# First layer norms in groups: one chain of vector instructions for the deviations of several token tiles

## The chip, the cores and the metric

The kernel runs on one core of one Trainium2 chip. Its engines work side by side, each through a queue of its own: PE (TensorE, matmuls and transposes into PSUM), DVE (VectorE), ACT (ScalarE), POOL (GpSimd) and SP (SyncE, which here only issues DMAs). The metric is the device time of one execution in microseconds (us). It was 1414.79 us before (median of three runs, 1411.76 to 1419.1).

## What is computed

One layer of a hybrid decoder over 1024 tokens of width 1024, with 256 memory tokens. Cut to what matters here:

```python
def layer_norm(x, g, b):
    mu = jnp.mean(x, axis=-1, keepdims=True)
    xc = x - mu
    var = jnp.mean(xc * xc, axis=-1, keepdims=True)
    return xc * lax.rsqrt(var + LN_EPS) * g + b

h = layer_norm(x, emb_ln_g, emb_ln_b)          # (1024, 1024): the first norms
mem_n = layer_norm(mem, mem_ln_g, mem_ln_b)    # (256, 1024)
z = h @ w_in                                   # feeds an S5 and a gated linear attention group
...                                            # output projection, cross-attention to mem_n, MLP
```

Everything after `z` (two mixers, cross-attention, a squared-ReLU MLP, three more norms) stays as it is.

## The kernel before

**Tiles.** Tokens lie in tiles of 128: eight of the sequence (`xs`, four to each of two arrays of 128 x 4 x 1024) and two of the memory (`mrow[:, 2]` and `mrow[:, 3]`). A tile has one token per partition and its 1024 features along the row. A mean or a deviation of such a tile is one number per partition: a column of 128 x 1.

**One norm.** `norm_stats` (line 211) reads the two halves of a tile with `bn_stats` (128x512 each), joins them with `bn_aggr` into `mv` (mean, variance), and calls `rsqrt1` (line 172), which finds the reciprocal root by a first guess in integers and three Newton steps: 2 `tensor_scalar` and 6 `scalar_tensor_tensor`, eight instructions of 128x1 that each need the one before. They write the tile `tq`; in the profile they stand as `tq<-mv` (first), `tq<-tq` int32 (second) and `tq<-tq` (the six). `layer_norm` (line 224) then applies it: on DVE (x - mean) * g, then * rstd + b for the left half; for the right half ACT scales with `tq` (for a "light" tile, seven of the eight by `LIGHT = 191`, with a bias that one more small DVE instruction, `tq<-mv,tq`, makes first), and POOL multiplies by g and adds b (`xs<-xs,row`).

**What surrounds it.** `embed(tk)` (line 461) normalises token tile tk, transposes its eight 128x128 blocks on PE, splits them into two parts of reduced precision (`h0T`: ACT the upper part, DVE the rest from PSUM), and stores the tile. `z_block` (line 413) multiplies a token tile by the weights `wr` on PE, 24 matmuls of 128x512; its epilogue `r_epi` uses ACT, DVE and POOL (`rt`). The loops at lines 470 and 505 run `embed(tk)` and `z_block(tk - 1)` in turn for eight tiles; the first four x tiles are loaded before, the next four within these loops. The norms of the memory (line 264) come first of all; then `mem_stream` (line 369) computes head 0 of the memory's projections, in which `mem_proj` splits `kvT` (ACT upper part, DVE the rest).

After the eight tiles come the projection of the gate's rank (line 525), `z_block(7)`, the weights `wu` (line 529; `weight`, line 190, loads `raw`, ACT makes the upper part `hl`, DVE or POOL the rest), and on DVE the parameters of the S5 group (lines 547 to 690, many instructions of 128x16 on `prm` and `par`). `par` takes the buffer of the rows g and b of the first norm, so that its first write waits for the last `xs<-xs,row`. The first product with `wu` is `z_fm` (line 873).

**What sets the order.** Tile dependencies are turned into semaphores, and the order of the instructions of each engine is laid out when the program is built, by program order and by the builder's own estimate of when operands are ready. So a queue holds small instructions of later code in what the builder took for gaps: in the trace the eight-instruction chains of two or three token tiles lie interleaved with other work. At run time each queue is worked through strictly in that order.

Of the kernel before, what the change touches and what calls it, by code (L numbers as in the profile page):

```python
# [7 lines left out]
F32 = mybir.dt.float32  # L8
F32R = mybir.dt.float32r
I32 = mybir.dt.int32  # L10
U8 = mybir.dt.uint8
AF = mybir.ActivationFunctionType
ALU = mybir.AluOpType
# [4 lines left out]
P = 128  # L18
D = 1024
SEQ = 1024  # L20
NT = SEQ // P
# [5 lines left out]
EPS = 1e-5  # L27
# [8 lines left out]
LIGHT = 191  # L36
# [45 lines left out]
def hybrid_layer(  # L82
# [9 lines left out]
    V = nc.vector  # L92
# [4 lines left out]
    x, mem, out = x[0], mem[0], out[0]  # L97
# [18 lines left out]
    small = ctx.enter_context(tc.tile_pool(name="small", bufs=4))  # L116
# [7 lines left out]
    def slot(name, shape, dtype=F32):  # L124
        return arena.tile(shape, dtype, tag="s", name=name)

    def bank(tag="d", shape=(P, 512)):
        return psp.tile(list(shape), F32, tag=tag, bufs={"d": 3, "s": 3, "g": 2}[tag], name="ps_" + tag)
# [6 lines left out]
    def ts(e, o, i, s1, s2=None, op0=ALU.mult, op1=None):  # L135
        if s2 is None:
            e.tensor_scalar(out=o, in0=i, scalar1=s1, scalar2=None, op0=op0)
        else:
            e.tensor_scalar(out=o, in0=i, scalar1=s1, scalar2=s2, op0=op0, op1=op1)  # L139

    def tt(e, o, a, b, op):
        e.tensor_tensor(out=o, in0=a, in1=b, op=op)  # L142

    def stt(e, o, a, s, b, op0, op1):
        e.scalar_tensor_tensor(out=o, in0=a, scalar=s, in1=b, op0=op0, op1=op1)  # L145

    def act(o, i, f=AF.Copy, **kw):
        A.activation(out=o, in_=i, func=f, **kw)  # L148
# [23 lines left out]
    def rsqrt1(y, v, eps, t):  # L172

        vh, w = t[:, 0:1], t[:, 1:2]
        ts(V, vh, v, eps, -0.5, ALU.add, ALU.mult)
        ts(V, y.bitcast(I32), vh.bitcast(I32), -0.5, 1597463007.0 - 2.0 ** 30 - 2.0 ** 22, ALU.mult, ALU.add)
        for _ in range(3):
            stt(V, w, y, vh, y, ALU.mult, ALU.mult)
            stt(V, y, w, 1.5, y, ALU.add, ALU.mult)

    ident = const.tile([P, P], F32, name="ident")
    G.memset(ident, 0.0)
    G.affine_select(out=ident, in_=ident, compare_op=ALU.not_equal, fill=1.0, base=0,
# [19 lines left out]
    def ln_rows(g, b):  # L203
        r = rowp.tile([P, 2, D], F32, tag="row", name="row")
        for i, v in enumerate((g, b)):
            if len(v.shape) == 1:
                v = v.rearrange("(o n) -> o n", o=1)
            nc.sync.dma_start(out=r[:, i, :], in_=v.to_broadcast([P, D]))
        return r

    def norm_stats(xt, st=None):

        mv = small.tile([P, 2], F32, tag="mv", name="mv")
        tq = small.tile([P, 4], F32, tag="tq", name="tq")
        half_done = st is not None
        if not half_done:
            st = small.tile([P, 2, 6], F32, tag="st", name="st")
        for i in range(1 if half_done else 0, 2):
            V.bn_stats(out=st[:, i, :], in_=xt[:, i * 512:(i + 1) * 512])
        V.bn_aggr(out=mv, in_=st)  # L220
        rsqrt1(tq[:, 0:1], mv[:, 1:2], EPS, tq[:, 1:3])
        return mv, tq

    def layer_norm(xt, rows, light=False, st=None):
        mv, tq = norm_stats(xt, st)
        lo_, hi_ = slice(0, 512), slice(512, D)
        if light:
            stt(V, xt[:, lo_], xt[:, lo_], mv[:, 0:1], rows[:, 0, lo_], ALU.subtract, ALU.mult)
            stt(V, tq[:, 3:4], mv[:, 0:1], -1.0, tq[:, 0:1], ALU.mult, ALU.mult)
            act(xt[:, hi_], xt[:, hi_], AF.Identity, scale=tq[:, 0:1], bias=tq[:, 3:4])  # L230
            tt(G, xt[:, hi_], xt[:, hi_], rows[:, 0, hi_], ALU.mult)
        else:
            stt(V, xt, xt, mv[:, 0:1], rows[:, 0, :], ALU.subtract, ALU.mult)
            act(xt[:, hi_], xt[:, hi_], scale=tq[:, 0:1])
        stt(V, xt[:, lo_], xt[:, lo_], tq[:, 0:1], rows[:, 1, lo_], ALU.mult, ALU.add)
        tt(G, xt[:, hi_], xt[:, hi_], rows[:, 1, hi_], ALU.add)

    def transposes(src_ap, dst):

        for b in range(2):  # L240
            pt = bank("s", (P, 4, P))
            for j in range(4):
                PE.transpose(pt[:, j, :], src_ap(4 * b + j), ident)
            hi, lo = dst(b)
            split(hi, lo, pt)
# [3 lines left out]
    mrow = slot("mrow", [P, 4, D])  # L249
# [11 lines left out]
    PE.transpose(gps[:, 0:16], gbr, ident[0:16, 0:16])  # L261
    act(gb, gps[:, 0:16])
    mps = [bank("sssd"[i], (P, 2, MEM)) for i in range(4)]
    for mt in range(2):
        xm = mrow[:, 2 + mt, :]
        mv, tq = norm_stats(xm)
        ts(V, xm[:, 0:512], xm[:, 0:512], mv[:, 0:1], tq[:, 0:1], ALU.subtract, ALU.mult)
        stt(V, tq[:, 3:4], mv[:, 0:1], -1.0, tq[:, 0:1], ALU.mult, ALU.mult)
        act(xm[:, 512:D], xm[:, 512:D], AF.Identity, scale=tq[:, 0:1], bias=tq[:, 3:4])
        for k in range(8):  # L270
            PE.transpose(mps[k // 2][:, k % 2, mt * P:(mt + 1) * P], xm[:, k * P:(k + 1) * P], ident)
    for b in range(4):
        z = (b + 1) % 3 * 512 + 512
        t = mrow[:, 0:2, :].rearrange("p a n -> p (a n)")[:, z:z + 512].rearrange("p (k m) -> p k m", k=2)
        for j in range(2):
            k = 2 * b + j
            if MT >> k & 1:
                act(t[:, j, :], mps[b][:, j, :], AF.Identity, scale=gb[:, k:k + 1], bias=gb[:, 8 + k:9 + k])
            else:
# [11 lines left out]
                  in_=lst[64:80, :].unsqueeze(2).to_broadcast([16, 2, 64]))  # L291
# [142 lines left out]
    xs = [slot("xs0", [P, 4, D])]  # L434
# [3 lines left out]
    rows = ln_rows(emb_ln_g, emb_ln_b)  # L438
# [12 lines left out]
    def r_epi(t, po):  # L451
# [6 lines left out]
        tt(eng(RE, t), th_, th_, ng, ALU.mult)  # L458
        srs.append(lambda: nc.scalar.dma_start(out=sr_d[t * P:(t + 1) * P, :], in_=th_))

    def embed(tk):
        xt = xs[tk // 4][:, tk % 4, :]
        layer_norm(xt, rows, LIGHT >> tk & 1)
        transposes(lambda k: xt[:, k * P:(k + 1) * P],
                   lambda b: tuple(h0T[b][hl][:, :, tk * P:(tk + 1) * P] for hl in range(2)))
        nc.scalar.dma_start(out=h0_d[tk * P:(tk + 1) * P, :], in_=xt)
# [3 lines left out]
    for tk in range(3):  # L470
        embed(tk)
        load_x(tk + 4)
        if tk == PP:
            pps = bank("g")
            PE.transpose(pps[:, 0:P], pm, ident)
            act(prm_s[:, 0:96], pps[:, 0:96])
            act(bglu, pps[:, 96:100], scale=0.5)
            act(bgate, pps[:, 100:102])

            cps = bank("g", (P, 2, 4, 64))  # L480
            for ri in range(2):
                for i in range(4):
                    for g in range(2):
                        PE.matmul(cps[64 * g:64 * g + 64, ri, i, :], cn[:, ri, i, :],
                                  ident.rearrange("p (j g h) -> p g j h", g=2, h=SH)[:, g], start=True, stop=True)
            act(prm_s[:, 2432:2944], cps.rearrange("p r i n -> p (r i n)"))
        if tk:
            z_block(wr, tok_block, tk - 1, r_epi)
# [85 lines left out]
    def exp_parts(z):  # L574

        zc, n, r, em, sc, kk = etmp
        ex, ex1 = pt(), pt()
        ts(e, zc, z, 88.0, -90.0, ALU.min, ALU.max)
        ts(e, n, zc, LOG2E, MAGIC, ALU.mult, ALU.add)
        ts(e, n, n, MAGIC, op0=ALU.subtract)  # L580
        stt(e, r, n, -LN2H, zc, ALU.mult, ALU.add)
        stt(e, r, n, -LN2L, r, ALU.mult, ALU.add)
        ts(e, em, r, 1.0 / 5040)
        for c in (1.0 / 720, 1.0 / 120, 1.0 / 24, 1.0 / 6, 0.5, 1.0):
            stt(e, em, em, c, r, ALU.add, ALU.mult)
# [15 lines left out]
    step, _ = exp_parts(ls)  # L601
# [35 lines left out]
    n = 1  # L637
# [311 lines left out]
    for s in LEVELS + (P,):  # L949
        w = 2 * SEQ // s  # L950
# [759 lines left out]
```

## Time and profile before

| | |
|---|---|
| median of three runs | 1414.79 us |
| the profiled execution: its own time, and the span from first to last instruction in it | 1412.6 us, 1410.8 us |
| mean granted TensorE clock in it | 0.986 |
| ACT, POOL busy | 570.1 us (40%), 460.0 us (33%) |
| moved over DMA | 199.81 MB, 142 GB/s |

The profile is of one execution. In the lists of instructions each row gives start, length, engine, line, operation, written tile <- read tiles, shape and count, and in brackets how long the engine had stood idle before and what released it. Most elementwise instructions are recorded in short helpers (L135 to L148), so groups are told apart by the names of their tiles. A window row gives, for each engine, busy time and count of instructions in a stretch of the span, then the granted clock of PE (1.00 is full speed), the share of the DMA engines and GB/s.

### The profile page before, as it was taken

The numbers are of one execution on the slowest core, as the hardware profiler recorded it, in microseconds if no ns is written. First come the engines' busy times: TensorE is split into PE (matmuls) and PEld (weight loads), VectorE is DVE, ScalarE is ACT, GpSimd is POOL, SyncE is SP. The second block draws the span as 40 slices with busy tenths as digits, with TensorE's granted clock in tenths as the row PEclk, the third lists the DMA queues.
The fourth block names the chain that finished last, engine by engine and source line by source line (L and its number), as shares of the span: only waits on it lengthen the run. The fifth ranks groups of instructions, "written<-read, shape, count | busy, mean of one in ns | idle before, by whom it ended". The sixth has DMA issues, their size and how long they took to land. (4 is left out here: it accounts for less than half of the span.)

```text
span 1410.8 us, 18927 instructions
## 1 busy us (share of the span) xinstructions
PE 1341.5 (95%) x6824; PEld 1112.6 (79%) x6824; DVE 998.0 (71%) x1783; ACT 570.1 (40%) x946; POOL 460.0 (33%) x338
## 2 busy tenths in 40 slices
PE   7798999999899998999998999999999999999997
PEld 6575788788898887788887777778888888888886
DVE  8999588756855489844478667766555676568797
ACT  4433532342545143333123654445545343335431
POOL 1663144312855133200014223443332142003364
PEclk9899999999999999999999999999999999999999
DMA  9722342543756120310120656554446985334432
GB/s 311 255 110 81 107 121 52 161 159 112 255 186 209 56 73 23 119 30 1 60 60 23 194 174 198 194 188 142 145 140 230 343 270 178 104 105 150 149 105 90
DMA packets 155513, 199.81 MB, mean 142 GB/s; under 512 B 16294, under 2 KB 86044, under 8 KB 155292
## 3 DMA queue, kind: packets, MB, share of 16 engines
q1 hardware_dynamic: 143536, 179.44, 39.5%
q10 hardware_dynamic: 11884, 19.17, 3.7%
q8 instruction: 54, 0.88, 0.3%
q14 instruction: 39, 0.32, 0.1%
HBM read 140.38 MB, written 58.20 MB: 141 GB/s over the span
## 5 line engine op out<-in xcount | busy, mean ns | idle before, releaser
L163 PE MATMUL ps_d<-xt,w1q 128*128 128x512 f32 x576 | 138.3, 391 | 9.8 <-DVE w1s L142 9.5
L163 PEld LDWEIGHTS ps_d<-xt,w1q 128*128 128x128 f32 x576 | 107.3, 188 | 35.4 <-issue 12.2
L142 POOL TENSOR_TENSOR hl<-raw,hl 128x1024 fp32r<-128x1024 f32 x21 | 63.0, 3006 | 168.3 <-ACT hl L148 168.2
L163 PE MATMUL ps_s<-cell 128*128 128x512 f32 x432 | 113.0, 389 | 0.0
L163 PE MATMUL ps_d<-cell 128*128 128x512 f32 x432 | 106.0, 389 | 0.4 <-DVE hid L142 0.4
L142 POOL TENSOR_TENSOR R<-R,row 128x512 f32<-128x512 f32 x42 | 57.8, 1386 | 138.4 <-ACT R L148 134.9
L163 PE MATMUL ps_d<-h0T,hl 128*128 128x512 f32 x384 | 93.6, 402 | 5.8 <-DVE hl L142 5.8
L163 PE MATMUL ps_g<-xb,w1q 128*128 128x512 f32 x384 | 94.3, 397 | 3.9 <-ACT hid L148 3.9
L163 PE MATMUL ps_d<-hl,y 128*128 128x512 f32 x384 | 95.1, 403 | 2.5 <-DVE y L142 2.5
L163 PEld LDWEIGHTS ps_d<-cell 128*128 128x128 f32 x432 | 81.0, 188 | 17.6 <-DVE hid L142 0.8
L163 PEld LDWEIGHTS ps_s<-cell 128*128 128x128 f32 x432 | 81.1, 188 | 16.8
L163 PEld LDWEIGHTS ps_d<-h0T,hl 128*128 128x128 f32 x384 | 73.2, 193 | 25.8 <-DVE hl L142 6.2
L163 PE MATMUL ps_d<-hl,h0T 128*128 128x512 f32 x384 | 91.1, 393 | 1.4 <-DVE h0T L142 1.3
L148 ACT ACTIVATE hl<-raw 128x1024 fp32r<-128x1024 f32 x62 | 64.8, 1059 | 66.1 <-PE ps_d L163 60.2
L163 PE MATMUL ps_d<-hl,p 128*128 128x512 f32 x384 | 89.0, 391 | 0.0
L163 PEld LDWEIGHTS ps_g<-xb,w1q 128*128 128x128 f32 x384 | 72.5, 191 | 19.6 <-ACT hid L148 4.7
L163 PEld LDWEIGHTS ps_d<-hl,y 128*128 128x128 f32 x384 | 72.6, 193 | 18.0 <-DVE y L142 3.0
L148 ACT ACTIVATE hid<-hid 128x512 f32<-128x512 f32 x112 | 70.8, 632 | 36.9 <-DVE hid L142 35.1
L163 PEld LDWEIGHTS ps_d<-hl,h0T 128*128 128x128 f32 x384 | 71.0, 188 | 17.3 <-DVE h0T L142 1.8
L163 PEld LDWEIGHTS ps_d<-hl,p 128*128 128x128 f32 x384 | 71.6, 188 | 14.6
L142 DVE TENSOR_TENSOR cell<-ha,cell 128x1024 fp32r<-128x1024 f32 x56 | 78.2, 1401 | 5.6 <-ACT cell L148 3.4
L148 ACT ACTIVATE w1q<-raw 128x512 fp32r<-128x512 f32 x80 | 50.0, 628 | 76.2 <-PE ps_d L163 39.6
(286 smaller groups left out, 2868.8 us busy)
## 6 DMA issues: line engine op xcount, KB each, us to landing
g_d<-hid SPq DMA_DIRECT2D x112, 256.0 KB
ha<-g_d SPq DMA_DIRECT2D x56, 512.0 KB
raw<-in_w_ff_dram SPq DMA_DIRECT2D x40, 512.0 KB
b<-in_w_ff_dram SPq DMA_DIRECT2D x32, 512.0 KB
raw<-in_w_mkv_dram SPq DMA_DIRECT2D x16, 512.0 KB
raw<-in_w_in_dram SPq DMA_DIRECT2D x16, 512.0 KB
wq<-in_w_mq_dram SPq DMA_DIRECT2D x8, 512.0 KB
xs<-in_x_dram SPq DMA_DIRECT2D x8, 512.0 KB
```

The costliest lines, as they stand in the source:

```text
L142: e.tensor_tensor(out=o, in0=a, in1=b, op=op)
L148: A.activation(out=o, in_=i, func=f, **kw)
L163: PE.matmul(o, lhs(i), rhs(j), start=first and n == 0, stop=last and n == 2, skip_group_check=more)
```

## The change

A second helper, `rsqrt_n`, does for n columns (128 x n) what `rsqrt1` does for one. A column cannot be the scalar operand of all n, so the fused instruction `y * vh * y` becomes two `tensor_tensor`: 2 `tensor_scalar`, 6 `tensor_tensor` and 3 `scalar_tensor_tensor`, eleven instead of eight. `norms_stats` makes the `bn_stats` and `bn_aggr` of several tiles (counts and shapes as before), then one such chain. It is called for the two memory tiles, and in `embed` at token tiles 0, 2 and 4, for tiles 0 and 1, 2 and 3, and 4 to 7. The later norms of the kernel go on calling `norm_stats`.

```diff
+    def rsqrt_n(y, v, eps, t):
+        n = y.shape[1]
+        vh, w = t[:, 0:n], t[:, n:2 * n]
+        ts(V, vh, v, eps, -0.5, ALU.add, ALU.mult)
+        ts(V, y.bitcast(I32), vh.bitcast(I32), -0.5, 1597463007.0 - 2.0 ** 30 - 2.0 ** 22, ALU.mult, ALU.add)
+        for _ in range(3):
+            tt(V, w, y, y, ALU.mult)
+            tt(V, w, w, vh, ALU.mult)
+            stt(V, y, w, 1.5, y, ALU.add, ALU.mult)
...
+    def norms_stats(xts):
+        n = len(xts)
+        mv = small.tile([P, 16], F32, tag="dg", bufs=2, name="mvn")[:, 0:8].rearrange("p (t c) -> p t c", c=2)
+        tq = small.tile([P, 12], F32, tag="sq", name="tqn")
+        for k, xt in enumerate(xts):
+            st = small.tile([P, 2, 6], F32, tag="st", name="st")
+            for i in range(2):
+                V.bn_stats(out=st[:, i, :], in_=xt[:, i * 512:(i + 1) * 512])
+            V.bn_aggr(out=mv[:, k], in_=st)
+        rsqrt_n(tq[:, 0:n], mv[:, 0:n, 1], EPS, tq[:, 4:4 + 2 * n])
+        return [(mv[:, k, 0:1], tq[:, k:k + 1], tq[:, 4 + k:5 + k]) for k in range(n)]
...
+    mem_known = norms_stats([mrow[:, 2 + mt, :] for mt in range(2)])
     for mt in range(2):
         xm = mrow[:, 2 + mt, :]
-        mv, tq = norm_stats(xm)
...
     def embed(tk):
         xt = xs[tk // 4][:, tk % 4, :]
-        layer_norm(xt, rows, LIGHT >> tk & 1)
+        if tk not in known:
+            same = range(tk, NT) if tk >= 4 else (tk, tk + 1)
+            known.update(zip(same, norms_stats([xs[i // 4][:, i % 4, :] for i in same])))
+        layer_norm(xt, rows, LIGHT >> tk & 1, known=known[tk])
```

In `layer_norm` the mean, the reciprocal root and the bias column are passed in as `known`; what it does with them is unchanged. The buffers of the new tiles are those of two tags that are next used much later (lines 1085 and 1166).

More of the change, by code (lines that the diff above doesn't have):

```diff
@@ L222, in norm_stats, with layer_norm @@
         return mv, tq
-    def layer_norm(xt, rows, light=False, st=None):
-        mv, tq = norm_stats(xt, st)
+    def norms_stats(xts):
[9 more added lines that the diff above has]
+        return [(mv[:, k, 0:1], tq[:, k:k + 1], tq[:, 4 + k:5 + k]) for k in range(n)]
+    def layer_norm(xt, rows, light=False, st=None, known=None):
+        if known is None:
+            mv, tq = norm_stats(xt, st)
+            known = mv[:, 0:1], tq[:, 0:1], tq[:, 3:4]
+        mean, rstd, nb = known
         lo_, hi_ = slice(0, 512), slice(512, D)
         if light:
-            stt(V, xt[:, lo_], xt[:, lo_], mv[:, 0:1], rows[:, 0, lo_], ALU.subtract, ALU.mult)
-            stt(V, tq[:, 3:4], mv[:, 0:1], -1.0, tq[:, 0:1], ALU.mult, ALU.mult)
-            act(xt[:, hi_], xt[:, hi_], AF.Identity, scale=tq[:, 0:1], bias=tq[:, 3:4])
+            stt(V, xt[:, lo_], xt[:, lo_], mean, rows[:, 0, lo_], ALU.subtract, ALU.mult)
+            stt(V, nb, mean, -1.0, rstd, ALU.mult, ALU.mult)
+            act(xt[:, hi_], xt[:, hi_], AF.Identity, scale=rstd, bias=nb)
             tt(G, xt[:, hi_], xt[:, hi_], rows[:, 0, hi_], ALU.mult)
         else:
-            stt(V, xt, xt, mv[:, 0:1], rows[:, 0, :], ALU.subtract, ALU.mult)
-            act(xt[:, hi_], xt[:, hi_], scale=tq[:, 0:1])
-        stt(V, xt[:, lo_], xt[:, lo_], tq[:, 0:1], rows[:, 1, lo_], ALU.mult, ALU.add)
+            stt(V, xt, xt, mean, rows[:, 0, :], ALU.subtract, ALU.mult)
+            act(xt[:, hi_], xt[:, hi_], scale=rstd)
+        stt(V, xt[:, lo_], xt[:, lo_], rstd, rows[:, 1, lo_], ALU.mult, ALU.add)
         tt(G, xt[:, hi_], xt[:, hi_], rows[:, 1, hi_], ALU.add)
@@ L263, in hybrid_layer @@
     mps = [bank("sssd"[i], (P, 2, MEM)) for i in range(4)]
+    mem_known = norms_stats([mrow[:, 2 + mt, :] for mt in range(2)])
     for mt in range(2):
         xm = mrow[:, 2 + mt, :]
-        mv, tq = norm_stats(xm)
-        ts(V, xm[:, 0:512], xm[:, 0:512], mv[:, 0:1], tq[:, 0:1], ALU.subtract, ALU.mult)
-        stt(V, tq[:, 3:4], mv[:, 0:1], -1.0, tq[:, 0:1], ALU.mult, ALU.mult)
-        act(xm[:, 512:D], xm[:, 512:D], AF.Identity, scale=tq[:, 0:1], bias=tq[:, 3:4])
+        mean, rstd, nb = mem_known[mt]
+        ts(V, xm[:, 0:512], xm[:, 0:512], mean, rstd, ALU.subtract, ALU.mult)
+        stt(V, nb, mean, -1.0, rstd, ALU.mult, ALU.mult)
+        act(xm[:, 512:D], xm[:, 512:D], AF.Identity, scale=rstd, bias=nb)
         for k in range(8):
@@ L459, in r_epi @@
         srs.append(lambda: nc.scalar.dma_start(out=sr_d[t * P:(t + 1) * P, :], in_=th_))
+    known = {}
     def embed(tk):
         xt = xs[tk // 4][:, tk % 4, :]
-        layer_norm(xt, rows, LIGHT >> tk & 1)
+        if tk not in known:
+            same = range(tk, NT) if tk >= 4 else (tk, tk + 1)
+            known.update(zip(same, norms_stats([xs[i // 4][:, i % 4, :] for i in same])))
+        layer_norm(xt, rows, LIGHT >> tk & 1, known=known[tk])
         transposes(lambda k: xt[:, k * P:(k + 1) * P],
```

## The prediction

> **What bounds the kernel now.** First the page's engine totals.
>
> ```profile
> PE 1341.5 (95%) x6824; PEld 1112.6 (79%) x6824; DVE 998.0 (71%) x1783; ACT 570.1 (40%) x946; POOL 460.0 (33%) x338
> ```
>
> PE is idle for 1410.8 - 1341.5 = 69.3 us in all, and only such idle time, or time at a low clock, can be won. The change touches nothing behind the first norms, so I ask next, by windows of 50 us, how much of it lies early.
>
> ```profile
> 0.00:50.00 50.00, 33.53 (x216) 30.17 (x217) 45.15 (x114) 24.11 (x39) 16.32 (x18) 0.90 0.86 282
> 50.00:100.00 50.00, 43.91 (x234) 35.61 (x233) 48.30 (x167) 18.59 (x33) 28.06 (x28) 1.00 0.54 194
> 100.00:150.00 50.00, 44.17 (x170) 30.51 (x169) 44.30 (x164) 20.43 (x27) 15.65 (x20) 0.93 0.28 90
> 150.00:200.00 50.00, 50.00 (x288) 39.28 (x289) 33.47 (x59) 20.49 (x34) 16.88 (x20) 1.00 0.34 103
> ```
>
> In the first 150 us PE lacks 28.4 us while DVE works 137.75 of 150; from 150 us on PE is full. So the opening is bound by DVE, and what PE gains there should reach the end, since a full PE follows. Third, PE's own waits in 0 to 150 us (us in total, times, longest):
>
> ```profile
> PE ps_d L163 <- DVE hl L142: 5.8, 1, 5.8
> ...
> PE ps_s L243 <- POOL xs L142: 4.8, 4, 2.4
> PE ps_d L163 <- DVE kvT L142: 4.4, 2, 4.2
> PE ps_s L271 <- DVE mrow L139: 3.8, 1, 3.8
> ```
>
> The largest is the last in time. The timeline shows what leads to it, and the windows what it does to the clock.
>
> ```profile
> 91.46 0.82 ACT L148 ACTIVATE xs<-xs,tq 128x512 f32<-128x512 f32 x1 [3.50 <-DVE tq L145]
> 92.35 2.69 POOL L142 TENSOR_TENSOR xs<-xs,row 128x512 f32<-128x512 f32 x2 [1.35 <-ACT xs L148]
> 95.07 0.43 DVE L561 COPY par<-prm 128x512 f32<-128x512 f32 x1 [0.34 <-POOL xs L142]
> 98.45 5.70 PE L163 MATMUL ps_d<-hl,h0T 128*128 128x512 f32 x24
> ...
> 123.66 1.21 DVE L142 TENSOR_TENSOR hl<-raw,hl 128x1024 fp32r<-128x1024 f32 x1
> 124.92 6.69 PE L163 MATMUL ps_d<-h0T,hl 128*128 128x512 f32 x16 [5.75 <-DVE hl L142]
> ```
>
> ```profile
> 44.00:50.00 6.00, 6.00 (x16) 4.75 (x17) 6.00 (x23) 1.43 (x3) 3.93 (x3) 0.59 0.62 150
> 119.00:125.00 6.00, 0.25 (x2) 0.09 (x1) 6.00 (x24) 0.00 (x0) 1.71 (x1) 0.92 0.00 0
> 125.00:131.50 6.50, 6.50 (x16) 4.89 (x16) 6.50 (x34) 0.00 (x0) 1.20 (x1) 0.55 0.72 237
> ```
>
> The last token tile's chain of small instructions holds ACT for 3.50 us; ACT and POOL then finish tile 7; its buffer becomes `par`, DVE starts the S5 parameters at 95.07 and reaches the weight split `hl` at 123.66. PE idles 5.75 us, and the clock granted behind it is 0.55: 16 matmuls take 6.69 us where 24 took 5.70, so 16 x 5.70 / 24 = 3.80 would do. **This place costs 5.75 + 2.89 = 8.6 us.**
>
> **The change, part by part.** DVE instructions of the chains in 18 to 96 us (the eight token tiles), then those of the memory in 4 to 11 us (count | busy us, mean ns):
>
> ```profile
> L145 DVE SCALAR_TENSOR_TENSOR tq<-tq 128x1 f32<-128x1 f32 x48 | 21.5, 468 | 0.0
> L219 DVE BATCH_NORM_STATS2 st<-xs 128x6 f32<-128x512 f32 x16 | 10.5, 669 | 0.0
> ```
>
> ```profile
> L145 DVE SCALAR_TENSOR_TENSOR tq<-tq 128x1 f32<-128x1 f32 x12 | 1.8, 184 | 0.1
> ```
>
> The same instruction means 184 ns early, with POOL at rest, and 468 ns later. The timeline shows why:
>
> ```profile
> 8.07 0.74 DVE L145 SCALAR_TENSOR_TENSOR tq<-tq 128x1 f32<-128x1 f32 x6
> ...
> 35.58 5.74 POOL L142 TENSOR_TENSOR hl<-raw,hl 128x1024 fp32r<-128x1024 f32 x2 [4.52 <-ACT hl L148]
> 36.70 2.33 DVE L145 SCALAR_TENSOR_TENSOR tq<-tq 128x1 f32<-128x1 f32 x1
> 39.55 1.78 DVE L145 SCALAR_TENSOR_TENSOR tq<-tq 128x1 f32<-128x1 f32 x1
> 41.28 6.73 POOL L142 TENSOR_TENSOR xs<-xs,row 128x512 f32<-128x512 f32 x4
> 41.38 1.18 DVE L145 SCALAR_TENSOR_TENSOR tq<-tq 128x1 f32<-128x1 f32 x1
> 43.20 0.68 DVE L142 TENSOR_TENSOR kvT<-ps_d,kvT 128x512 fp32r<-128x512 f32 x1
> ```
>
> One column takes up to 2.33 us beside POOL and ends as POOL does: 39.55 + 1.78 = 41.33, and POOL's pair 35.58 + 5.74 = 41.32. Of the 21.5 us, 48 x 0.184 = 8.8 is work and **12.7 us is waiting for POOL**.
>
> *Count.* Tokens: 8 x 8 = 64 small instructions become 3 x 11 = 33. Spacing unhindered is 0.74 / 6 = 0.12 us, less where chains interleave; I take 0.10: 31 x 0.10 = 3.1 us of DVE.
> *Waits.* The two-input ones go from 48 to 3 x 9 = 27. If waits go by count, 12.7 x 21 / 48 = 5.6 us. Bounds: 0 (the next two-input instruction takes each wait over) and 12.7. I take 5.6, between: what often stands behind a chain instruction doesn't wait for POOL (`bn_stats` means 669 over the stretch, kvT from PSUM takes 0.68 beside POOL), so not every wait has an heir.
> *Wider columns.* No token norm has 128 x n now. The nearest rows, from 350 to 520 us:
>
> ```profile
> L145 DVE SCALAR_TENSOR_TENSOR sq<-sq 128x4 f32<-128x4 f32 x24 | 4.9, 205 | 0.6
> L142 DVE TENSOR_TENSOR sq<-sq 128x4 f32<-128x4 f32 x12 | 2.5, 204 | 0.4
> ```
>
> Four columns cost what one does; added cost 0, at most 33 x (0.205 - 0.184) = 0.7 us.
> *Together* DVE reaches the weight split 3.1 + 5.6 = 8.7 us earlier, between 2.4 and 15.8. The 16 `bn_stats` stay. PE needs DVE 5.75 earlier there, so the wait closes; I leave 0.5 for PE's own shifts: **-5.2**, and with so short a wait the low clock goes: **-2.9** (PE's wait of 2.4 us for `xs` has 1.00 around it). For DVE to use this, tile 7 must end sooner than 95.07: its deviation is then known with tile 4's, and the 3.50 us of ACT's wait go; ACT and POOL are next, and POOL has 28.06 of 50 busy there.
>
> *Order.* Each first tile now waits for the last of its group. Tiles 0 and 1: PE is on `mem_proj` then, hidden. Tile 4 is the exposed one:
>
> ```profile
> 73.35 0.82 ACT L148 ACTIVATE xs<-xs,tq 128x512 f32<-128x512 f32 x1 [1.45 <-DVE tq L145]
> 74.24 3.46 POOL L142 TENSOR_TENSOR xs<-xs,row 128x512 f32<-128x512 f32 x2 [1.30 <-ACT xs L148]
> ...
> 77.75 0.66 PE L243 MATMUL ps_s<-ident,xs 128*128 128x128 f32 x4 [2.37 <-POOL xs L142]
> ```
>
> Ahead of its bias come two more `bn_stats` (1.3 us), and the interleaved chains of tiles 5 and 6 drop out; ACT, POOL and PE follow it in turn. I take +1, bounds -1 and +4; against it stand PE's later waits for `xs`, about 1 us, which go because tiles 5 to 7 are known early. Sum 0. Memory: 16 small instructions become 11, but tile 0 waits for tile 1; 0, within 0.5 either way. kvT: PE's wait of 4.2 us is DVE's queue of three chain instructions (2.33 + 1.78 + 1.18 = 5.3 us) ahead of 43.20; which ones stand there afterwards depends on the builder: 0, bounds -5.3 and +5.4 (below). DMA: the loads stay; those behind freed buffers move with DVE.
>
> **Sum**, against the profiled execution: 1412.6 - 5.2 - 2.9 = 1404.5 us. The median shown, 1414.8, is 2.2 higher; I say **1405.5**, between 1404.5 and 1406.7.
>
> **Rivals.**
> *The waits stay (25%).* POOL's work is unchanged and each of its instructions may hold up some two-input one. For: the three long waits quoted fall on POOL instructions that stand back to back. Against: from 50 to 100 us POOL is idle 50 - 28.06 = 21.9 us, so an instruction moved there often meets none. DVE gains 2.4 to 3.1 us, the wait at 119 shrinks to about 3, and the low clock may stay: 1412.6 - 2.9 = 1409.7, up to 1413 if the builder's new order spends it.
> *kvT is pushed back (15%): slower.* Tiles 2 and 3 now have one chain of nine two-input instructions, each behind the other, and POOL runs without a pause from 35.58 to 41.28 + 6.73 = 48.01. If that chain is queued ahead of kvT, each link waits for one POOL end, and kvT moves from 43.20 to about 48.6: +5.4, at low clock all the while. It decides once more than three links stand ahead of kvT. If DVE then gains nothing, 1418; if the wait at 119 absorbs it, about 1412.
> *kvT comes free (15%).* None of the three stands there: -4.2, and 16 matmuls at a clock of 0.59 in 44 to 50 us run faster by up to 6.0 - 3.8 = 2.2: 1404.5 - 6.4 = 1398.
> *Even widths take the lock too (5%).* One column in a `tensor_scalar` does not wait today; two columns elsewhere do (ns min/median/max):
>
> ```profile
> L139 DVE TENSOR_SCALAR tq<-mv x8: 134/140/143, 21.3 to 85.3; 128x1 f32<-128x1 f32 x8
> ```
>
> ```profile
> L137 DVE TENSOR_SCALAR sm<-sm x16: 154/168/1384, 583.7 to 675.3; 128x2 f32<-128x2 f32 x16
> ```
>
> Six `tensor_scalar` of the new chains would each wait up to 1.2 us: 7.2 off the 8.7, and 1411. The Trainium skill, "SBUF — State Buffer", section "Who interferes with whom", names the mechanism: a DVE instruction in a two-port mode, or with two SBUF inputs against a POOL read, blocks fully until the other ends; an even count lets `tensor_scalar` into such a mode. The 1384 agrees; the 128x1 never over 143 does too.
>
> **How the numbers follow.** Forecast 40%, its own range 1401 to 1410; the rivals 25, 15, 15 and 5. The range 1396 to 1417 leaves out the far end of the two kvT cases. About 0.5% (7 us) is what a measurement of this kernel tells from none: below 1407.7 lie most of the forecast (35) and kvT free (15), so faster 0.50; above 1421.9 only a pushed kvT with a late tile 4 (+4), and orders that I do not foresee, 0.11; the rest, 0.39, within.
>
> **What would show it.** Right: `tq` chains of 33 small instructions in 18 to 96 us with under 10 us of waiting; the copy into `par` before 90; PE's wait for `hl` near 119 under 2 us and a clock of 1.00 after it. Wrong: other DVE rows (`prm`, `xs`, `hl`) grown by what `tq` lost; kvT after 45; PE's wait for `xs` of tile 4 over 5 us, with a low clock behind it. If the opening is shorter by 8 us and the end is not, something behind 150 us has given it back, against my reading that a full PE carries it through.

## The result, and the profile after

The changed kernel takes 1423.83 us (median of 19 runs) where the kernel before takes 1416.38 beside it: a ratio of **1.0053, interval 1.0035 to 1.0070**. It is slower by half a per cent, above the forecast of 1405.5 and above the whole range. A second comparison (`after_again`, below) gives 1.0055.

First the page's totals of the changed kernel, then its windows of 50 us (PE, PEld, DVE, ACT and POOL busy, the clock granted to PE, share of the DMA engines, GB/s):

```profile
PE 1344.5 (95%) x6824; PEld 1113.6 (78%) x6824; DVE 998.0 (70%) x1747; ACT 570.6 (40%) x946; POOL 455.8 (32%) x338
```

```profile
0.00:50.00 50.00, 32.84 (x228) 29.91 (x229) 44.09 (x87) 23.75 (x35) 15.00 (x17) 0.93 0.85 281
50.00:100.00 50.00, 42.49 (x192) 33.70 (x191) 43.62 (x130) 18.25 (x34) 21.51 (x17) 0.90 0.55 180
100.00:150.00 50.00, 45.26 (x182) 32.23 (x182) 46.79 (x189) 17.73 (x25) 20.06 (x32) 0.93 0.27 93
```

DVE did become less busy: in 50 to 100 us its idle time went from 50 - 48.30 = 1.7 us to 50 - 43.62 = 6.4. But PE did not become busier: 43.91 us before, 42.49 now. What was saved on DVE turned into DVE waiting. PE's own waits in 0 to 150 us say for what (us in total, times, longest):

```profile
PE ps_s L270 <- DVE xs L145: 6.3, 1, 6.3
PE ps_d L163 <- DVE hl L142: 5.5, 2, 4.7
...
PE ps_s L299 <- DVE mrow L139: 4.6, 1, 4.6
PE ps_s L270 <- POOL xs L142: 3.0, 2, 2.8
```

The wait of 4.2 us for `kvT` is gone from the list (0.2 now), the one for `hl` near 119 us has shrunk only from 5.75 to 4.7, and a new one of 6.3 us stands first: for tile 0's left half, which did not make PE wait before. The timeline of DVE, PE and POOL around it, in the changed kernel:

```profile
28.68 2.23 DVE L139 TENSOR_SCALAR tqn<-mvn 128x2 f32<-128x2 f32 x1
...
36.45 2.31 DVE L145 SCALAR_TENSOR_TENSOR tqn<-tqn 128x2 f32<-128x2 f32 x1
38.68 0.15 DVE L139 TENSOR_SCALAR tqn<-tqn 128x2 int32<-128x2 int32 x1
38.79 2.53 DVE L142 TENSOR_TENSOR tqn<-tqn 128x2 f32<-128x2 f32 x4
...
41.56 0.74 DVE L145 SCALAR_TENSOR_TENSOR xs<-xs,tqn,row 128x512 f32<-128x512 f32 x1
...
45.17 0.68 DVE L142 TENSOR_TENSOR kvT<-ps_d,kvT 128x512 fp32r<-128x512 f32 x1
```

```profile
28.48 2.40 POOL L142 TENSOR_TENSOR wo<-raw,wo 128x1024 fp32r<-128x1024 f32 x1 [22.25 <-ACT wo L148]
35.89 5.15 POOL L142 TENSOR_TENSOR hl<-raw,hl 128x1024 fp32r<-128x1024 f32 x2 [5.01 <-ACT hl L148]
```

```profile
42.36 1.11 PE L270 MATMUL ps_s<-ident,xs 128*128 128x128 f32 x4 [6.27 <-DVE xs L145]
```

Before, PE transposed tile 0 from 35.05 us on; its left half had been done at 33.13. Now it is done at 42.30. Tile 0's chain now also carries tile 1, three of its links (28.68, 36.45 and the first of those at 38.79) each wait until a POOL instruction ends (28.48 + 2.40 = 30.88 and 28.68 + 2.23 = 30.91 are one moment), and the transposes stand in PE's queue ahead of the products with `kvT`.

To follow this through the span I take the start of the same matmul in both traces (the nth of its kind): `x16` behind the wait for `hl`, for instance, starts at 124.92 before and at 129.60 now, +4.7. The table gives these differences, PE's **lag** against the profile of before, at four places of before's span. Each row is from one profile; the two pairs of profiles of one kernel differ by 0.9 and 1.4 us at 161, so a lag is good to about 1 us.

| kernel | ratio to before (interval) | 36 us | 44 us | 90 us | 161 us |
|---|---|---|---|---|---|
| whole change | 1.0053 (1.0035 to 1.0070) | +7.9 | +3.3 | +6.0 | +4.6 |
| after_again | 1.0055 (1.0035 to 1.0074) | +8.9 | +4.3 | +7.0 | +5.5 |
| g_mem | 1.0029 (1.0012 to 1.0045) | +1.1 | +6.2 | +4.1 | +5.3 |
| g_pairs | 1.0035 (1.0015 to 1.0056) | +7.2 | +4.7 | +2.4 | +3.9 |
| g_4567 | 0.9974 (0.9954 to 0.9994) | +0.1 | +0.2 | +2.7 | -4.7 |
| g_4567_again | 0.9978 (0.9958 to 0.9998) | +0.1 | -0.1 | +2.4 | -3.3 |
| mem_pairs | 1.0036 (1.0022 to 1.0050) | +9.4 | +4.5 | -0.1 | +2.3 |
| b_fill | 0.9980 (0.9960 to 1.0000) | +0.1 | -3.1 | -2.9 | -2.5 |
| mem_fill | 0.9983 (0.9968 to 0.9998) | +1.1 | -1.6 | -4.3 | -3.2 |
| pairs_fill | 0.9991 (0.9973 to 1.0010) | +2.5 | -1.5 | -3.4 | -1.9 |
| after_fill | 1.0008 (0.9993 to 1.0024) | +3.7 | -2.2 | +1.2 | -0.4 |
| after_t7 | 1.0034 (1.0014 to 1.0053) | +9.2 | +5.0 | +8.7 | +4.2 |
| pairs_ts1 | 1.0008 (0.9991 to 1.0025) | +6.7 | +2.1 | -1.9 | -2.0 |
| g_45_67 | 1.0005 (0.9989 to 1.0021) | 0.0 | -0.2 | +3.2 | -1.2 |
| g_567 | 1.0026 (1.0008 to 1.0044) | 0.0 | +1.1 | +1.7 | -1.1 |
| g_4567_m7 | 1.0035 (1.0017 to 1.0052) | 0.0 | -3.9 | +3.5 | +1.7 |
| b_links3 | 1.0012 (0.9994 to 1.0030) | +0.1 | +5.0 | +2.4 | +1.4 |

In the whole change PE is 7.9 us late at 36, 3.3 at 44 (the products with `kvT`), 6.0 at 90, and ends the opening 4.6 late. A count of the products recorded under L163 goes the same way: by 64 us PE has begun 197 of them where before had begun 204, by 90 us 266 against 283. In `mem_pairs`, which leaves out the group of four, it is 196 by 64 and 283 by 90, so that what is lost between 64 and 90 is lost with that group. The time lost is 0.53% of 1416, 7.5 us; the rest lies behind 200 us (last section).

### The profile page after: what moved, and what is told of

It is laid out like the page before. It is cut to its first block, busy times and chain, and to the rows that moved or that the text cites. A ratio compares the mean times of both kernels' runs of the same rounds, so it can differ in the third digit from the quotient of the medians.

```text
span 1419.1 us, 18882 instructions
## 1 busy us (share of the span) xinstructions
PE 1344.5 (95%) x6824; PEld 1113.6 (78%) x6824; DVE 998.0 (70%) x1747; ACT 570.6 (40%) x946; POOL 455.8 (32%) x338
## 5 line engine op out<-in xcount | busy, mean ns | idle before, releaser
L163 PE MATMUL ps_d<-xt,w1q 128*128 128x512 f32 x576 | 138.7, 391 | 9.7 <-DVE w1s L142 9.7
L163 PEld LDWEIGHTS ps_d<-xt,w1q 128*128 128x128 f32 x576 | 107.2, 188 | 36.0 <-issue 12.2
L163 PE MATMUL ps_s<-cell 128*128 128x512 f32 x432 | 113.1, 389 | 0.0
L163 PE MATMUL ps_d<-cell 128*128 128x512 f32 x432 | 106.0, 389 | 0.1
L163 PE MATMUL ps_d<-h0T,hl 128*128 128x512 f32 x384 | 93.5, 401 | 4.7 <-DVE hl L142 4.7
L163 PE MATMUL ps_g<-xb,w1q 128*128 128x512 f32 x384 | 94.2, 397 | 3.9 <-ACT hid L148 3.9
L163 PE MATMUL ps_d<-hl,y 128*128 128x512 f32 x384 | 95.3, 403 | 2.5 <-DVE y L142 2.5
L163 PE MATMUL ps_d<-hl,h0T 128*128 128x512 f32 x384 | 94.8, 405 | 0.0
L163 PEld LDWEIGHTS ps_d<-cell 128*128 128x128 f32 x432 | 81.0, 188 | 17.3 <-DVE hid L142 0.5
L163 PEld LDWEIGHTS ps_s<-cell 128*128 128x128 f32 x432 | 81.1, 188 | 16.8
L163 PEld LDWEIGHTS ps_d<-h0T,hl 128*128 128x128 f32 x384 | 73.1, 193 | 24.8 <-DVE hl L142 5.2
L163 PE MATMUL ps_d<-hl,p 128*128 128x512 f32 x384 | 89.0, 391 | 0.0
L163 PEld LDWEIGHTS ps_g<-xb,w1q 128*128 128x128 f32 x384 | 72.5, 191 | 19.6 <-ACT hid L148 4.7
L163 PEld LDWEIGHTS ps_d<-hl,y 128*128 128x128 f32 x384 | 72.5, 193 | 18.0 <-DVE y L142 2.9
L163 PEld LDWEIGHTS ps_d<-hl,h0T 128*128 128x128 f32 x384 | 73.9, 195 | 16.1 <-issue 0.6
L163 PEld LDWEIGHTS ps_d<-hl,p 128*128 128x128 f32 x384 | 71.6, 188 | 14.6
```

The costliest lines, as they stand in the source:

```text
L163: PE.matmul(o, lhs(i), rhs(j), start=first and n == 0, stop=last and n == 2, skip_group_check=more)
```

## The experiments

**Which part of the change costs?** Each of the three places alone, and the whole once more. In the code `embed` then calls `norms_stats` only for the groups named, and other tiles take their own chain as before:

```diff
-        if tk not in known:
-            same = range(tk, NT) if tk >= 4 else (tk, tk + 1)
-            known.update(...)
-        layer_norm(xt, rows, LIGHT >> tk & 1, known=known[tk])
+        for same in ((4, 5, 6, 7),):
+            if tk == same[0]:
+                known.update(zip(same, norms_stats([xs[i // 4][:, i % 4, :] for i in same])))
+        layer_norm(xt, rows, LIGHT >> tk & 1, known=known.get(tk))
```

`g_mem` (memory alone): 

> Only the two memory tiles are grouped; the eight token tiles are as before. In the profile of the changed kernel PE is 0.9 us behind the kernel before at the same matmuls from 20 to 31 us. Theory (the group of four is the loss): 0.9 us late there and hidden by PE's wait for kvT at 38 to 44 us, so ratio 0.999 to 1.001. Rival (the 128x2 instructions that wait for POOL are the loss): the same, since POOL rests there. Rival (each group costs its serial chain): +0.9 us kept to the end, 1.0006.

`g_pairs` (tokens 0 and 1, 2 and 3): 

> Only token tiles 0 and 1, 2 and 3 are grouped; memory and tiles 4 to 7 as before. Theory (the group of four is the loss): 0.998 to 1.001, and PE at the first product of z_block(4) not later than before. Rival (two-column instructions that wait for POOL, 2.23 us for one tensor_scalar at 28.7 us): 1.003 to 1.005, PE's wait near 36 to 42 us over 6 us and kept to 160 us. Rival (each group costs its serial chain): about 1.002.

`g_4567` (tokens 4 to 7): 

> Only token tiles 4 to 7 are grouped; memory and tiles 0 to 3 as before. Theory (the group of four is the loss): 1.003 to 1.006; tile 4's scale on ACT 5 us or more later than 73.35, the first write of par near 103 instead of 95, PE 4 to 6 us late at 160 us. Rival (two-column instructions): 0.998 to 1.001. Rival (each group costs its serial chain): about 1.002.

`after_again` (the whole change): 

> The changed kernel once more, for a second profile. If the opening decides, PE is again 4 to 6 us behind the kernel before at 160 us, and the later 3.5 us (at 370 to 382 us, where the first profile had a wait of 2.0 us for vst on ACT) come or go from run to run. If that later place belongs to the change, it is there again. Ratio 1.003 to 1.007.

The theory that the group of four loses the time fell. Memory and pairs lose by themselves, and the group of four **gains**. For the pairs the rival of two-column instructions that wait for POOL gave the right size (1.0035, and 6.3 us of waiting for tile 0); for memory (1.0029) and for the group of four (0.9974) every range written down was missed. The group's PE timeline, behind the place where before waited 5.75 us and then took 6.69 us for 16 matmuls at a clock of 0.55, and the window there:

```profile
124.41 2.56 PE L163 MATMUL ps_d<-h0T,hl 128*128 128x512 f32 x10 [1.58 <-DVE hl L142]
```

```profile
125.00:131.50 6.50, 6.50 (x27) 4.53 (x26) 6.50 (x28) 3.84 (x5) 2.94 (x3) 1.00 0.60 202
```

A wait of 1.58 and a clock of 1.00: a gain at the place that the forecast named exists, 4.7 us at 161, in the group of four alone (its second profile, below, has less of it). In `g_pairs` DVE's timeline, and POOL's beside it, show the early loss:

```profile
36.41 2.30 DVE L145 SCALAR_TENSOR_TENSOR tqn<-mvn,tqn 128x1 f32<-128x1 f32 x1
38.64 2.92 DVE L145 SCALAR_TENSOR_TENSOR xs<-xs,tqn,row 128x512 f32<-128x512 f32 x1
41.48 1.22 DVE L145 SCALAR_TENSOR_TENSOR tqn<-mvn,tqn 128x1 f32<-128x1 f32 x1
42.62 0.74 DVE L145 SCALAR_TENSOR_TENSOR xs<-xs,tqn,row 128x512 f32<-128x512 f32 x1
43.29 1.23 DVE L145 SCALAR_TENSOR_TENSOR tqn<-tqn 128x2 f32<-128x2 f32 x1
44.55 2.29 DVE L142 TENSOR_TENSOR tqn<-tqn 128x2 f32<-128x2 f32 x1
...
47.90 0.68 DVE L142 TENSOR_TENSOR kvT<-ps_d,kvT 128x512 fp32r<-128x512 f32 x1
```

```profile
35.74 5.27 POOL L142 TENSOR_TENSOR hl<-raw,hl 128x1024 fp32r<-128x1024 f32 x2 [4.17 <-ACT hl L148]
40.96 3.53 POOL L142 TENSOR_TENSOR xs<-xs,row 128x512 f32<-128x512 f32 x2
44.47 2.36 POOL L142 TENSOR_TENSOR hl<-raw,hl 128x1024 fp32r<-128x1024 f32 x1
```

POOL runs five instructions end to end (ends at 38.70, 41.01, 42.69, 44.50 and 46.82), and five of the six two-input instructions of DVE shown end with one of them; only the one at 42.62 slips between. `kvT` leaves at 47.90 where it left at 43.20. PE is 4.7 us late there, 2.4 at 90 and 3.9 at 161; by which steps it gets from the one to the other is not shown. In `g_mem`, whose token tiles are coded as before, the queue behind the memory came out otherwise, five such waits stand ahead of `kvT`, and it leaves at 49.43.

**Take POOL's reads away.** POOL fills the low parts of three pieces of `wr` with zeros; applied to before, memory alone, pairs alone, and the whole:

```diff
+        if e is None:
+            act(hl[:, 0], raw)
+            G.memset(hl[:, 1].bitcast(F32), 0.0)
...
-    wr = [wcols(w_in, 2 * kp, 1536, eng(MWR, kp)) for kp in range(4)]
+    wr = [wcols(w_in, 2 * kp, 1536, V if kp == 2 else None) for kp in range(4)]
```

`b_fill`: 

> The kernel before, except that POOL fills the low parts of three of the four weight pieces wr with zeros (it writes and reads nothing) instead of computing them from raw and hl; the fourth piece stays on DVE. So the low part of wr is left out. Theory (DVE's two-input instructions wait for POOL instructions that read): the three chain instructions of 2.33, 1.78 and 1.18 us ahead of kvT shrink to 0.2 to 0.5 us each wherever they don't meet the pair xs<-xs,row, and kvT stands 2 to 4 us sooner than 43.20; the time falls to between 1405 and 1413. Rival (DVE's queue is late by its work, not by its waits): kvT stays between 42.5 and 43.5, time within 0.2% of before.

`mem_fill`: 

> The memory's group alone, with the same fill in place of POOL's three splits of wr. Theory (the group is slower because its instructions moved beside POOL's splits): against b_fill the loss of 0.29% goes, ratio to b_fill 0.999 to 1.001; PE's delay against b_fill at its first product with kvT is under 1.5 us (6.2 with the splits). Rival (the memory's chain itself is late, 1 us at 20 us of the span, and the queue orders that follow from it): ratio to b_fill 1.002 to 1.004, PE late by 4 us or more at kvT.

`pairs_fill`: 

> The pairs of tokens 0 and 1, 2 and 3 alone, with the same fill. Theory: the instructions after the chain (tqn<-mvn,tqn 2.30, xs<-xs,tqn,row 2.92 us beside the splits) fall to their unhindered lengths (under 0.3 and about 0.7), PE's wait for tile 0's xs falls from 6.3 to under 3, ratio to b_fill 0.998 to 1.001. Rival (tile 0 is late because it waits for tile 1's statistics and for eleven links): PE's wait stays over 5 us, ratio to b_fill 1.002 to 1.004.

`after_fill`: 

> The whole change with the same fill. Theory: against b_fill only the group of four is left to be seen, which alone gave 0.9974: ratio to b_fill 0.996 to 0.999, PE's waits before 50 us no longer than b_fill's by over 2 us in sum. Rival (order and length of the chains, not POOL): ratio to b_fill 1.003 to 1.006, as with the splits.

In `b_fill` the three links ahead of `kvT` take 0.14, 0.19 and 0.15 us where they took 2.33, 1.78 and 1.18, and `kvT` leaves at 39.03, 4.2 us sooner: a little more than expected. The time, 1413.29, is just above its range.

Against `b_fill` the medians are 1413.31 for memory, 1415.55 for the pairs and 1416.57 for the whole: 1.000, 1.0016 and 1.0023, each good to about 0.2%. The memory's loss is gone, as the theory said. The lag of the pairs at 161, against `b_fill`, is 0.6 us where it was 3.9, so that loss is explained for the most part; the ratio lies between the two ranges written down. So does that of the whole, which was to gain by the theory. The fill is also shorter than the split (0.95 us, where a split takes about 2.4), so these runs show that POOL's splits cost the time, and not yet whether it is their reading or their length. PE's wait for tile 0 in `pairs_fill`, and what released it:

```profile
37.49 0.66 PE L274 MATMUL ps_s<-ident,xs 128*128 128x128 f32 x4 [2.20 <-DVE xs L145]
```

So of 6.3 us some 4 were POOL and 2.2 are tile 0 waiting for tile 1. The whole change keeps a loss of its own: against `b_fill` PE is 4.1 us late at 90 (+1.2 against -2.9) and 2.1 at 161 (-0.4 against -2.5), where with the splits it was 6.0 and 4.6. So about half of its lag at 161 has nothing to do with the splits of `wr`.

**Does the group of four still gain inside the whole?** `mem_pairs` is the whole change without it. 

> The memory's group and the two pairs, tokens 4 to 7 as before: the whole change without its group of four. Theory (the whole loss is made before 50 us, and the group of four still gains behind it): slower than the whole change, ratio 1.006 to 1.008. Rival (with the first two parts ahead of it the group of four doesn't gain but costs: PE went from 2 us ahead at 64 us to 6 us behind at 90 in the whole change): ratio 1.000 to 1.003, PE's delay against before under 3 us at 90 us.

It comes out on the rival's side (just above its band; no lag at 90 us): 1.0036 and +2.3 at 161, against 1.0053 and 1.0055 and about +5 with the group. The intervals overlap. What is shown is that the group's gain is gone: alone it makes PE 3.3 to 4.7 us sooner, and a gain of that size would have put the whole change near 1.001. That it costs 2 to 3 us behind the other two rests on the lags of single profiles. The changed kernel's timeline shows what it meets there, on ACT, POOL and DVE:

```profile
80.77 2.14 ACT L148 ACTIVATE xs<-xs,tqn 128x512 f32<-128x512 f32 x3 [3.32 <-DVE tqn L145]
...
97.55 0.60 ACT L148 ACTIVATE rt<-ps_d 128x512 f32<-128x512 f32 x1 [6.62 <-PE ps_d L163]
98.04 1.08 ACT L148 ACTIVATE h0T<-ps_s 128x512 fp32r<-128x512 f32 x2
99.00 0.83 ACT L148 ACTIVATE xs<-xs,tqn 128x512 f32<-128x512 f32 x1
```

```profile
81.57 7.55 POOL L142 TENSOR_TENSOR xs<-xs,row 128x512 f32<-128x512 f32 x5 [2.03 <-ACT xs L148]
```

```profile
80.82 0.15 DVE L145 SCALAR_TENSOR_TENSOR tqn<-mvn,tqn 128x1 f32<-128x1 f32 x1
...
81.62 3.47 DVE L145 SCALAR_TENSOR_TENSOR xs<-xs,tqn,row 128x512 f32<-128x512 f32 x2
85.01 1.21 DVE L145 SCALAR_TENSOR_TENSOR tqn<-mvn,tqn 128x1 f32<-128x1 f32 x1
86.15 1.84 DVE L145 SCALAR_TENSOR_TENSOR xs<-xs,tqn,row 128x512 f32<-128x512 f32 x1
...
102.95 0.43 DVE L594 COPY par<-prm 128x512 f32<-128x512 f32 x1 [2.83 <-POOL xs L142]
```

Three things stand here. Tile 4's bias comes at 80.82 (73.01 before, 78.27 in `g_4567`). All four tiles are then released at once, and three of DVE's four last steps fall on POOL's run of five; the same burst is in `g_4567`, which gains all the same, so it does not tell the two apart. And tile 7, known since 80.7, is scaled at 99.00: ACT's queue has it behind `rt`, which waits 6.62 us for PE. So the copy into `par` moves from 95.07 to 102.95, the wrong way; in `g_4567` tile 7 was scaled at 88 and the copy came at 92.70.

**Put tile 7 ahead of that wait.** Its norm is applied with tile 6's:

```diff
+        if tk != NT - 1:
             layer_norm(xt, rows, ...)
+        if tk == NT - 2:
+            layer_norm(xs[1][:, 3, :], rows, LIGHT >> NT - 1 & 1, known=known[NT - 1])
```

`after_t7`: 

> The whole change, with the norm of tile 7 applied together with that of tile 6, one step of the loop sooner in the program (its transposes stay). In ACT's queue its scaling then stands ahead of the rt and the two h0T that wait 6.62 us for PE, not behind them; before 70 us nothing moves. Theory (the group's gain at 119 us is lost because tile 7, though its deviation is known, is scaled only at 99.00, so that par starts at 102.95): the scaling stands at 87 to 94, the copy into par before 97, PE's wait for hl near 119 falls from 4.7 to under 2.5, ratio to before 1.000 to 1.003. Rival (the wait at 119 stays because PE and DVE are both late from 28 to 48 us on): wait over 4, ratio 1.004 to 1.006.

Not shown to help. PE's wait for `hl` there falls from 4.7 to 2.8, but every figure misses the theory's range: the wait was to be under 2.5, the scaling comes at 96.30 and not by 94, the copy into `par` at 101.46 and not before 97, and 1.0034 cannot be told from 1.0053. And the wait is shorter because PE comes later, 8.3 us behind before at 119 where the whole change was 5.7 behind: the matmuls behind `hl` start at 130.35, against 129.60 and 130.56 in the two profiles of the whole change.

**Is it the even width?** The `tensor_scalar` of the pairs one column at a time:

```diff
-        ts(V, vh, v, eps, -0.5, ALU.add, ALU.mult)
+        for c in range(n):
+            ts(V, vh[:, c:c + 1], v[:, c:c + 1], eps, -0.5, ALU.add, ALU.mult)
```

`pairs_ts1`: 

> The two pairs alone, with the two tensor_scalar of the chain made one column at a time (four of 128x1 in place of two of 128x2). Theory (a wait for POOL is not saved but passed on: whichever next instruction has two SBUF inputs takes it): the tensor_scalar stay under 0.2 us each, the first tensor_tensor behind them grows by what they lose, PE's wait for tile 0's xs stays at 5.5 to 7, ratio 1.002 to 1.005. Rival (the even width itself is the cost): PE's wait falls by 2 us or more, ratio 1.000 to 1.002.

The width is not it. Already in `g_pairs` and in the second profile of the whole change no `tensor_scalar` of the pairs is held (0.15 to 0.17 us), and PE's wait for tile 0 (6.3 and 7.2 us) and the ratio are no better. In `pairs_ts1` none is held either, the third link has a wait (1.80 us), and PE's wait for tile 0 stays at 5.85, as the theory said. Yet the ratio is 1.0008, below what it gave: in the new queue three such waits stand ahead of `kvT` and not five, and it leaves at 43.96 where `g_pairs` had 47.90. A few more instructions reordered the queue; that the order is worth the difference to 1.0035 is likely but not shown, as the two intervals overlap.

**Push kvT alone.** Three links ahead of its split in the kernel before:

```diff
+        for _ in range(links):
+            stt(V, o[:, 1, 0, 0:1], o[:, 0, 0, 0:1].bitcast(F32), 1.0, o[:, 0, 0, 1:2].bitcast(F32), ALU.mult, ALU.add)
```

`b_links3`: 

> The kernel before with three more instructions of 128x1 on DVE, each with two SBUF inputs and each needing the one before, that write into one number of kvT's lower part ahead of its split (which then overwrites it). Unhindered they are 0.4 us of work. Theory (each such link ahead of kvT waits for one POOL end): kvT goes from 43.20 to between 46 and 49, PE is 2.5 us or more late at its products with kvT, and the ratio is 1.001 to 1.004. Rival (what a link costs there is its own 0.15 us, and the losses of the groups come from elsewhere): kvT before 45, ratio 0.999 to 1.001.

`kvT` goes to 48.19 and PE is 5.0 us late at 44: the number came as expected, but the mechanism only in part, so there is luck in it. Of the three links one waits (2.29 us), the others take 0.15; the rest of the delay is other work that now stands ahead of `kvT` or waits longer there, among it a split of `hl` (1.22). By 161 us only 1.4 is left, and 1.0012 is not told from 1. So a late `kvT` alone does not make the losses of `g_mem` and `g_pairs` at the end (5.3 and 3.9); what else in their queues does was not taken apart.

**Is the gain of the group of four firm, and can it be had more cheaply?** The same kernel again; two groups of two; tile 4 left out; and POOL's first two splits of `wr` on DVE (`MWR = 4` to `7`):

`g_4567_again`: 

> The group of four alone once more, the same kernel. Theory (its gain is real: PE 4.67 us sooner from 124 us on, because the wait for hl fell from 5.75 to 1.6): ratio 0.995 to 0.999 again, PE 4 to 5.5 us sooner at 160 us. Rival (the first comparison drew fast runs): ratio 0.999 to 1.002.

`g_45_67`: 

> Only tokens 4 and 5, and 6 and 7, as two pairs; all else as before. Theory (what gains is that tile 7's deviation is known early, what costs is tile 4 waiting for three more tiles): tile 4's bias nb stands at 75 to 77 (73.01 before, 78.27 with the group of four), PE's wait for hl under 3, ratio 0.995 to 0.999. Rival (the gain needs one chain for all four, since each further chain meets POOL again): PE's wait for hl over 4, ratio 0.999 to 1.002.

`g_567`: 

> Only tokens 5, 6 and 7 in a group; tile 4 has its own chain as before. Theory (the group of four gains by knowing tile 7 early and loses by making tile 4 wait): tile 4's bias within 1 us of 73.01, PE late by under 1.5 us at 90 us (2.65 with the group of four), its wait for hl under 2.5 us, ratio 0.993 to 0.998. Rival (ACT scales tile 7 late again, since its scaling stands behind tile 6's store and transposes): wait for hl over 3.5, ratio 0.998 to 1.001.

`g_4567_m7`: 

> The group of four alone, and POOL's first two splits of wr moved to DVE (POOL keeps the last). Theory (POOL's splits from 35 to 41 us cost DVE more in waits, 2.33 and 1.78 and 1.18 us, than the two splits cost on DVE, 2.4 us): kvT at or before 43.2, PE not later than with the group of four alone at 60 us, ratio 0.993 to 0.998, below 0.9974. Rival (DVE's added work is what is late): PE later by 2 us or more at 44 us, ratio 0.998 to 1.003.

It repeats (0.9978), and is the one version here with nothing left out that beats both kernels: 1414.5 and 1413.24 us where before took 1416.08 and 1417.35 beside it. In the second profile the gain is almost all in the clock:

```profile
124.39 3.96 PE L163 MATMUL ps_d<-h0T,hl 128*128 128x512 f32 x16 [3.10 <-DVE hl L142]
```

Against the 124.92, 6.69 and 5.75 of before PE comes 2.1 us later to this wait, leaves it 0.5 sooner, and needs 2.7 us less for the same 16 matmuls. None of the variants keeps the gain. With two pairs PE's wait for `hl` is 2.9, as expected, but the 16 matmuls behind it take 5.51 us; tile 4's bias comes at 79.04, later than expected, and the opening gains 1.2 us only. (In `after_t7` they take 5.53 behind a wait of 2.84. So the length of the wait alone does not decide the clock; what else does is open.) With tile 4 left out of the group its bias still comes at 76.15, not near 73, and PE's wait for `hl` is 4.7. With the splits on DVE `kvT` is sooner (38.58; PE 3.9 us ahead at 44), and PE is 3.5 late at 90. The ratios of `g_567` and `g_4567_m7`, 1.0026 and 1.0035, miss the ranges of theory and rival alike. Both are also slower than their lag at 161 allows, by 3 to 5 us. Between 370 and 400 us their lag grows by about 3, and with it that of seven of the other profiles, the two of the whole change among them; in the remaining eight it grows by less than 0.5. In just these nine the 16 matmuls behind a wait for `kvT` there take 5.3 to 6.8 us, in the other eight and in before 3.9 (6.79 in `g_567`, where the granted clock is 0.50 from 375 to 380 us and 1.00 before). The wait ahead of them is over 1.6 us in eight of the nine and under 1.6 in all the rest, but only 0.7 in `after_again`, the ninth; what makes the clock low there is open.

## Why the prediction was wrong

*DVE's saving: right in size, wrong in what became of it.* The groups of DVE's instructions in 18 to 106 us of the changed kernel:

```profile
L145 DVE SCALAR_TENSOR_TENSOR xs<-xs,tqn,row 128x512 f32<-128x512 f32 x8 | 9.0, 1138 | 0.0
L142 DVE TENSOR_TENSOR tqn<-tqn 128x2 f32<-128x2 f32 x12 | 6.3, 545 | 0.1
L145 DVE SCALAR_TENSOR_TENSOR tqn<-tqn 128x2 f32<-128x2 f32 x6 | 3.0, 514 | 0.1
L139 DVE TENSOR_SCALAR tqn<-mvn 128x2 f32<-128x2 f32 x2 | 2.4, 1197 | 0.0
L145 DVE SCALAR_TENSOR_TENSOR tqn<-mvn,tqn 128x1 f32<-128x1 f32 x7 | 2.1, 304 | 0.0
L142 DVE TENSOR_TENSOR tqn<-tqn 128x4 f32<-128x4 f32 x6 | 2.1, 343 | 0.0
```

With four small rows (1.2 us) the 33 chain instructions take 6.3 + 3.0 + 2.4 + 2.1 + 1.2 = 15.0 us, where the 64 of before (18 to 96 us) took 21.5 + 2.2 (its `tensor_scalar`) = 23.7: 8.7 us less, which is the 3.1 + 5.6 forecast. But the waits have heirs: `xs<-xs,tq,row` went from 6.9 to 9.0, the bias from 1.0 to 2.1, and the 17 `tensor_scalar` on `prm` from 2.7 to 4.9. That is 5.4 us given back (0.8 comes off `xs<-xs,mv,row`), and I had argued that not every wait has an heir. That the saving comes out as 8.7 is an agreement of the sum; its two terms were not measured apart.

*The step that failed is "Order".* It summed to 0, and the profile shows each term:
- "Tiles 0 and 1: PE is on `mem_proj` then, hidden": PE waits 6.3 us for tile 0, because its transposes stand ahead of the `kvT` products and its links ahead of POOL's run of splits. Nothing in the quoted rows said that they had slack; before it was 1.9 us (done at 33.13, taken at 35.05).
- Tile 4, "+1, bounds -1 and +4": its bias is 7.8 us later (80.82 against 73.01) and PE is 6.0 late at 90, where `mem_pairs`, the same without this group, is level (-0.1). Alone it was inside the bounds, +2.7.
- Memory "0, within 0.5": in `g_mem` PE is 1.1 late at 36 us, and the queue that follows is another; +5.3 at 161.
- kvT "0, bounds -5.3 and +5.4": 43.20 to 45.17 in the whole, 47.90 and 49.43 in the parts. The rival of a pushed `kvT` was right about how (more than three links ahead of it), and its 15% was too little; but the price at the end is not its 5.4: in `b_links3`, which pushes `kvT` alone, 1.4 of 5.0 us is left at 161.

*The wait at 119 us and the clock: a right place, not reached.* -5.2 and -2.9 were forecast; in the whole the wait shrinks by 1.0, and the matmuls behind it are as slow as they were (6.58 us; 6.69 before):

```profile
129.60 6.58 PE L163 MATMUL ps_d<-h0T,hl 128*128 128x512 f32 x16 [4.74 <-DVE hl L142]
```

"ACT and POOL are next" was the place to look harder: the ACT queue put tile 7 behind PE, at 99.00. In `g_4567` the low clock goes in both profiles, and the wait falls to 1.58 and 3.10. That "with so short a wait the low clock goes" is not borne out as a rule: behind 2.84 and 2.87 us it stayed low.

*"The opening is bound by DVE"* was read from shares, and that was the deeper fault. PE, DVE, ACT and POOL wait for each other in turn there, and each queue has one order. Taking 8.7 us from DVE's work shifts which of them is late, and where it lands depends on the queue that the builder lays out. "From 150 us on PE is full" was read too far as well: it holds for the window shown, but of the 69.3 us that PE is idle before, only 28.4 lie ahead of 150 us (PE works 44.52 of 50 from 550 to 600, for one).

*Even widths* (5%): seen in one of the two profiles of the whole change, once in six `tensor_scalar` (28.68, 2.23 us). The Trainium skill, "SBUF — State Buffer", section "Who interferes with whom", says that a `tensor_scalar` in a two-port mode contends with POOL, and an instruction with two SBUF inputs only with a POOL instruction that reads. `pairs_fill` agrees, with one case of each: a two-input link inside POOL's first fill, which only writes, takes 0.14 us, and a `tensor_scalar` of two columns beside the second ends with it (34.89, and the fill 34.86).

```profile
31.62 0.95 POOL L209 MEMSET hl<- 128x1024 f32 x1
33.91 0.95 POOL L209 MEMSET hl<- 128x1024 f32 x1 [1.33 <-PE ps_d L163]
32.23 0.14 DVE L142 TENSOR_TENSOR tqn<-tqn 128x2 f32<-128x2 f32 x1
33.99 0.90 DVE L139 TENSOR_SCALAR tqn<-mvn 128x2 f32<-128x2 f32 x1
```

## What to carry to other kernels

Joining chains saves instructions, but makes the first member wait for the last and releases all members at once; count the slack of the first and what the burst meets before counting the saving. Where POOL ran without a pause here, most of the small two-input DVE instructions waited for the end of a POOL instruction, so count how many of them stand ahead of the next thing that PE needs, and not how many there are. And an engine that is over 90% busy in a stretch is not its bound until one has shown that nothing else is nearly late there: apply a change place by place, since here one place gained and two lost.

## What the runs showed that was not expected

A single chain of dependent links took 0.19 us a link even with POOL at rest: the memory's 11 links of 128x2 in the changed kernel, first and last below, run from 7.19 to 9.32 us, where the two chains of before, interleaved, started an instruction each 0.12 us. So 11 instructions in place of 16 gave no earlier result here.

```profile
7.19 0.17 DVE L139 TENSOR_SCALAR tqn<-mvn 128x2 f32<-128x2 f32 x1
...
9.16 0.16 DVE L145 SCALAR_TENSOR_TENSOR tqn<-tqn 128x2 f32<-128x2 f32 x1
```

Behind 200 us, ACT waits 4.3 to 4.8 us for a store of `vst` near 385 us in `g_pairs` and the whole change, and PE 1.5 to 2.0 for ACT. Six of the eight profiles in which tokens 0 to 3 are in pairs show PE's wait, the other two (`after_fill` and `after_t7`) don't, and no profile without those pairs shows more than 0.2. In the same six the 16 matmuls near 375 us take 5.3 to 5.6 us, in those two 3.9, so the two go together. It may be part of the 2 to 3 us that the whole change loses behind 200 us, beside these matmuls (5.36 us in the whole, 3.90 before); the cause of neither was tried.
